# Products that fill half of TensorE's array, gathered into fewer bursts, in a one-core hybrid SSD and attention layer

## The chip, the core and the metric

The kernel runs on one core of a Trainium2 chip. The metric is the device time of one execution in microseconds (us), of which the median of three runs is given. The core has five instruction queues that meet only at semaphores: TensorE (PE, matrix products into PSUM; its weight loads are shown as PEld), VectorE (DVE), ScalarE (ACT), GpSimd (POOL) and SyncE (SP, which here issues nearly all DMAs). Each takes its instructions in the order in which they are written into its queue.

## The reference, cut to what matters

One layer on 512 tokens of width 1024, float32. `u = x @ w_in` is split into the inputs of two branches:

```python
# branch A, per direction; groups g = 4, heads per group r = 8, chunks c of 128 tokens
y_diag = einsum('bgcls,bgrcls,bcsgrp->bclgrp', cb, lmat, xc)     # within a chunk
y_off  = einsum('bclgn,bcgrpn,bgrcl->bclgrp', cc, prev, exp(a_cs))  # from the states before it
y = (y_f + y_b + d_skip * xh) * silu(z)        # both directions; then RMSNorm per group, @ w_proj_ssd
# branch B: 12 heads of width 64, windows with dilation 1, 4 and 16
o = einsum('bdhinm,bdhime->bdhine', softmax(q @ k.T / 8 - slope * dist), v)   # @ w_proj_attn
h = layer_norm(alpha * x + (sigmoid(gA) * A + sigmoid(gB) * B) @ w_out)
out = layer_norm(alpha * h + square(relu(h @ w_up)) @ w_down)
```

A head is 64 wide, and the array has 128 rows and 128 columns. So a product that sums over one head's width (the scores q k) fills 64 rows, and one that makes one head's output (y, and the products of softmax weights and values) fills 64 columns. The two heads of a pair are issued alternately, one on each half.

## The kernel before

The wide products (w_in, the projections, the two layers of the MLP) are made of 128 x 128 by 128 x 512 steps, each taken three times from a high and a low part of both operands (`mm3`, lines 136 to 138). The weights come from HBM through `Stream`: a DMA to `wraw`, ACT makes the high part `wh` (line 110), DVE the low part `wl` (line 111), with two buffers of `wh` and `wl`.

**SSD stage** (about 78 to 498 us). For each of four groups, `ssd(g)` runs beside a list of projection tiles (`tile_task`). Both are Python generators that yield an estimate of their time; `run` takes steps from the one that is behind, and this alone sets the order on TensorE (`tc.manual_schedule`). The order on the other engines is made by the framework's scheduler when the program is built.

In `ssd(g)` four pairs of heads follow each other (`pr`, each with tile `j = 4g + pr`). A pair loads two `bc` tiles and one `be` tile by DMA, makes the state products `ps_yo` (line 483) that DVE multiplies into `be` (lines 484 to 486), POOL adds the two directions' parts (line 487), and `head` builds each head's decay matrix `G1`, with four buffers (lines 444 to 465). One pair later, `y_out` (line 353) multiplies it by the transposed `x` (line 360: 8 products, 128 x 64 by 128, in the trace 16 records) into a PSUM tile of tag `y`, of which there are two. DVE adds `D * x` (line 362, into a tile `yt`), POOL adds `be` (line 363), DVE multiplies by the gate (line 364), ACT squares (line 366) and POOL sums the squares (line 368). The fourth pair's `y_out` waits in `late` for the next group's start.

**Attention stage** (498 to 590 us). `attention()` runs beside the projection tiles of branch A (`ps_pa`). Score products for the near window (line 628): for each of two tiles `i` of q and k, two bursts `bp` of four products, into two PSUM tiles each, `bp = 0` of tag `tp` (three buffers) and `bp = 1` of tag `y` (two buffers); then DVE adds the bias out of PSUM into `pt` (line 636), and takes maxima (line 637) and their negatives (line 639); ACT makes the exponentials. The scores with dilation (line 658) are four bursts of eight products, one for each of the tiles 2 to 5, loaded into the two buffers of q and k by `load_qk`. The score tiles are read from PSUM by DVE alone.

Then the weights are transposed on TensorE and multiplied with the values: `class_v` (line 716, 16 products, one burst for each `i`) and `near_v` (line 744, 4 products for each of four blocks `b`). `later()` issues what the previous step left in `todo`, so a burst of value products follows each set of transposes. Blocks 0 and 3 of `near_v` have two products whose sum runs over 64 rows only. The copies `tt` of the transposes rotate through six buffers.

Of the kernel before, what the change touches and what calls it, by code (L numbers as in the profile page):

```python
# [45 lines left out]
def hybrid_layer_kernel(ctx: ExitStack, tc: tile.TileContext, t: dict, out: bass.AP):  # L46
# [303 lines left out]
        for j in range(4 * g, 4 * g + 4):  # L350
            dve.scalar_tensor_tensor(ys[j], ys[j], vec[:, V_NW + j:V_NW + j + 1], ps, op0=ALU.mult, op1=ALU.mult)

    def y_out(g, pr, xt, ms, be, sqs):

        j = 4 * g + pr
        py = ps_tile("y", f"ps_y{j}", 2)
        for c in range(NCH):
            for hh in range(2):
                hs = slice((pr * 2 + hh) * HD, (pr * 2 + hh + 1) * HD)
                pe.matmul(py[hh * HD:(hh + 1) * HD, ch(c)], xt[c][:, hs], ms[hh][:, ch(c)], start=True, stop=True)  # L360
        yt = sp.tile([P, S], F32, name=f"yt{j}", tag="acc", bufs=2)
        dve.scalar_tensor_tensor(yt, fm["x", j], vec[:, V_DSK + j:V_DSK + j + 1], py, op0=ALU.mult, op1=ALU.add)
        pool.tensor_add(yt, yt, be[:, 0, :])
        dve.tensor_mul(ys[j], ys[j], yt)
        sq = sp.tile([P, S], F32, name=f"sq{j}", tag="sq", bufs=2)
        act.activation(sq, ys[j], AF.Square)
        if pr:
            pool.tensor_add(sq, sq, sqs[-1])
        sqs.append(sq)
        tail[g] = sq  # L370

    late = [None]

    def ssd(g):
# [17 lines left out]
            cb.append(cbm)  # L392
        yield 3.0 if g else 10.0
        if late[0]:
            y_out(*late[0])
        yield 1.5
        xt = []
        for c in range(NCH):
# [45 lines left out]
        def head(pr, hh, bcs):  # L444

            h = g * 8 + pr * 2 + hh
            U = sp.tile([P, S], F32, name=f"U{h}", tag="U", bufs=2)
            G1 = sp.tile([P, S], F32, name=f"G1_{h}", tag="G1", bufs=4)
            for c in range(NCH):
                act.activation(U[:, ch(c)], bcs[1][:, hh, ch(c)], AF.Identity, bias=acr[:, c, 32 + h:33 + h])  # L450
            for c in range(NCH):
                dve.scalar_tensor_tensor(U[:, ch(c)], bcs[0][:, hh, ch(c)], acr[:, c, h:h + 1], U[:, ch(c)], op0=ALU.subtract, op1=ALU.min)  # L452
            act.activation(U, U, AF.Exp)
            for c in range(NCH):
                act.activation(G1[:, ch(c)], cb[0][:, c, :], AF.Copy, scale=tok[:, c, h:h + 1])
# [12 lines left out]
        pend = None  # L468
        for pr in range(4):
            h0 = g * 8 + pr * 2  # L470
            j = 4 * g + pr
# [13 lines left out]
            dve.tensor_mul(be[:, 0, :P], be[:, 1, :P], po[1][:, :P])  # L485
            dve.tensor_mul(be[:, 1, P:S - P], be[:, 1, P:S - P], po[1][:, P:S - P])
            pool.tensor_add(be[:, 0, P:S - P], be[:, 0, P:S - P], be[:, 1, P:S - P])
            ms = []
            with tc.issue_after(ins.ins):
                ms.append(head(pr, 0, bcs))  # L490
            yield 7.0
            if pend:
                y_out(*pend)
            ms.append(head(pr, 1, bcs))
            yield 7.0
            pend = (g, pr, xt, ms, be, sqs)
# [73 lines left out]
    def attention():  # L570
# [23 lines left out]
        tts = [ap.tile([P, 4, P], F32, name=f"tt{n}", tag="tt", bufs=2) for n in range(2)]  # L594
# [22 lines left out]

        for i in range(2):
            qf, kf = qk[i]
            for bp in range(2):  # L620
                pss = pair_tiles(bp, f"ps_s0_{i}{bp}")
                for bb in range(2):
                    b = bp * 2 + bb
                    k0, k1 = kr[b]
                    o = k0 - (P * b - 64)
                    for hh in range(2):
                        pr = slice(hh * HD, (hh + 1) * HD)
                        pe.matmul(pss[hh][:, bb * 256 + o:bb * 256 + o + k1 - k0], qf[pr, b * P:(b + 1) * P], kf[pr, k0:k1], start=True, stop=True)
                for hh in range(2):
                    jj = 2 * i + hh  # L630
                    for bb in range(2):
# [6 lines left out]
                        nm = nm0[:, b, jj:jj + 1]  # L638
                        dve.tensor_scalar(nm, st0[:, b, 0, jj:jj + 1], -1.0, None, op0=ALU.mult)
                        act.activation(pt[:, :w], pt[:, :w], AF.Exp, bias=nm, accum_out=st0[:, b, 1, jj:jj + 1])  # L640
                yield 3.5
        dma.dma_start(vc, dr_v.rearrange("(i r) d -> i r d", r=4)[:, :, 0:512])
        dma.dma_start(v0[:, 1:4, :], dr_v[64:448, 512:768].rearrange("(c p) d -> p c d", p=P))
        dma.dma_start(v0[0:64, 0, :], dr_v[0:64, 512:768])
        dma.dma_start(v0[0:64, 4, :], dr_v[448:512, 512:768])
        dma.dma_start(dr_st.rearrange("(b p) m -> p b m", p=P), st0.rearrange("p b a j -> p b (a j)"))
        for gg in range(2):
            for i in range(2):
                tl = 2 + gg * 2 + i
                tile_qk(tl)  # L650
                load_qk(tl)
                qf, kf = qk[tl]
                pss = pair_tiles(i, f"ps_s{tl}")
                for r in range(4):
                    rs = slice(r * P, (r + 1) * P)
                    for hh in range(2):
                        pr = slice(hh * HD, (hh + 1) * HD)
                        pe.matmul(pss[hh][:, rs], qf[pr, rs], kf[pr, rs], start=True, stop=True)
                for hh in range(2):
                    jj = i * 2 + hh  # L660
                    pt = ptc[gg, jj]
# [99 lines left out]
        for i in range(2):  # L761
# [431 lines left out]
```

## Time and profile before

| | |
|---|---|
| median of three runs | 1011.24 us (1010.66 to 1011.32) |
| the profiled execution: time | 1010.76 us |
| its span in the profile | 1008.9 us |
| TensorE busy | 999.4 us (99%) |
| TensorE weight loads busy | 827.1 us |
| VectorE busy | 733.3 us (73%) |
| ScalarE busy | 548.3 us (54%) |
| GpSimd busy | 73.7 us (7%) |
| mean granted clock | 0.998 |

The profile is of one execution; rows below are from it, in us from the start of its span. Matmuls overlap, so the time that a matmul takes up is read from the distance between starts, and not from its duration. In a row of the timeline, neighbours of one kind are merged, with their count at the end.

### The profile page before, as it was taken

How to read it: one execution, taken by the hardware profiler on the slowest of the kernel's cores; microseconds unless marked ns; L12 is line 12 of the kernel's file. 1: busy time of each engine (PE TensorE's matmuls, PEld its weight loads, DVE VectorE, ACT ScalarE, POOL GpSimd, SP SyncE). 2: the span in 40 equal slices, each digit the busy share in tenths (PEclk: the TensorE clock that was granted, in tenths of full speed). 3: DMA queues.
4: the chain of work that ended last, by engine and by line, in shares of the span. 5: the costliest groups of instructions: out<-in, count | busy, mean ns of one | idle time of the engine just before them, and what ended most of it. 6: DMA issues, size and time to landing. Idle time of an engine off the chain costs nothing.

```text
span 1008.9 us, 13601 instructions
## 1 busy us (share of the span) xinstructions
PE 999.4 (99%) x5073; PEld 827.1 (82%) x5073; DVE 733.3 (73%) x1108; ACT 548.3 (54%) x1026; POOL 73.7 (7%) x66
## 2 busy tenths in 40 slices
PE   9999999999999999999999999999999999999997
PEld 7888888888888888888778778898888888888886
DVE  4296978679878996986698267564676886787457
ACT  4454787368857884765765444214544545454330
POOL 0000202220221122213000000000000000000000
PEclk9999999999999999999999999999999999999999
DMA  7435355434652555365774249414234314311222
GB/s 241 151 130 157 99 190 174 140 108 138 197 171 91 175 190 165 122 204 168 251 220 115 73 160 309 149 43 149 81 104 126 105 46 162 107 48 56 84 84 84
DMA packets 48450, 140.43 MB, mean 139 GB/s; under 512 B 6528, under 2 KB 7424, under 8 KB 48128
## 3 DMA queue, kind: packets, MB, share of 16 engines
q1 hardware_dynamic: 48240, 139.30, 43.4%
q8 instruction: 40, 0.66, 0.3%
q10 hardware_dynamic: 144, 0.26, 0.1%
q14 instruction: 26, 0.21, 0.1%
HBM read 128.25 MB, written 11.30 MB: 138 GB/s over the span
## 4 chain that ended last, share of the span: by engine, by line
PE 89%; DVE 5%; DMA 2%; ACT 2%; issue 1%; POOL 0%; DVEq 0%; SPq 0%; ACTq 0%; POOLq 0%
PE ps_u L137 6%; PE ps_u L138 6%; PE ps_u L136 6%; PE ps_p L136 4%; PE ps_p L138 4%; PE ps_p L137 4%; PE ps_pa L136 3%; PE ps_z L136 3%; PE ps_z L138 3%; PE ps_z L137 3%; PE ps_pa L137 3%; PE ps_pa L138 3%; PE ps_x L136 3%; PE ps_x L138 2%; PE ps_x L137 2%; PE ps_yo L483 2%
## 5 line engine op out<-in xcount | busy, mean ns | idle before, releaser
L111 DVE TENSOR_TENSOR wl<-wraw,wh 128x1024 fp32r<-128x1024 f32 (+1 forms) x141 | 172.0, 1223 | 123.1 <-ACT wh L110 118.7
L110 ACT CAST wh<-wraw 128x1024 fp32r<-128x1024 f32 (+1 forms) x141 | 145.9, 1039 | 192.4 <-PE ps_u L137 89.0
L137 PE MATMUL ps_u<-htl,wh 128*128 128x512 f32 (+1 forms) x288 | 105.3, 366 | 0.3 <-DVE htl L906 0.3
L136 PE MATMUL ps_u<-hth,wh 128*128 128x512 f32 (+1 forms) x288 | 105.3, 366 | 0.0
L138 PE MATMUL ps_u<-hth,wl 128*128 128x512 f32 (+1 forms) x288 | 105.2, 365 | 0.0
L1000 DVE TENSOR_TENSOR cl<-wq,ch 128x1024 fp32r<-128x1024 f32 x42 | 51.3, 1223 | 29.3 <-ACT ch L999 29.2
L136 PE MATMUL ps_p<-ch,ah 128*128 128x512 f32 x168 | 65.4, 389 | 0.0
L137 PE MATMUL ps_p<-cl,ah 128*128 128x512 f32 x168 | 65.4, 389 | 0.0
L138 PE MATMUL ps_p<-ch,al 128*128 128x512 f32 x168 | 65.4, 389 | 0.0
L137 PEld LDWEIGHTS ps_u<-htl,wh 128*128 128x128 f32 x288 | 54.3, 189 | 9.2 <-DVE htl L906 0.5
L138 PEld LDWEIGHTS ps_u<-hth,wl 128*128 128x128 f32 x288 | 54.3, 189 | 8.8
L136 PEld LDWEIGHTS ps_u<-hth,wh 128*128 128x128 f32 x288 | 54.2, 189 | 8.8 <-ACT hth L905 0.3
L999 ACT CAST ch<-wq 128x1024 fp32r<-128x1024 f32 x42 | 44.1, 1052 | 21.4 <-PE ps_p L138 21.4
L452 DVE SCALAR_TENSOR_TENSOR U<-bc,acr,U 128x128 f32<-128x128 f32 x128 | 45.9, 392 | 8.8 <-ACT U L450 8.7
L136 PE MATMUL ps_pa<-yh,wh 128*128 128x512 f32 x128 | 52.1, 407 | 0.0
L136 PE MATMUL ps_g<-xh,wh 128*128 128x512 f32 x128 | 51.5, 402 | 0.0
L136 PE MATMUL ps_x<-xh,wh 128*128 128x512 f32 x128 | 50.9, 398 | 0.0
L136 PE MATMUL ps_z<-xh,wh 128*128 128x512 f32 x128 | 50.9, 398 | 0.0
L137 PE MATMUL ps_pa<-yl,wh 128*128 128x512 f32 x128 | 50.1, 392 | 0.2 <-DVE yl L563 0.2
L138 PE MATMUL ps_g<-xh,wl 128*128 128x512 f32 x128 | 50.0, 391 | 0.1
L138 PE MATMUL ps_pa<-yh,wl 128*128 128x512 f32 x128 | 50.1, 391 | 0.0
L138 PE MATMUL ps_x<-xh,wl 128*128 128x512 f32 x128 | 50.1, 391 | 0.0
(289 smaller groups left out, 2444.7 us busy)
## 6 DMA issues: line engine op xcount, KB each, us to landing
wraw<-in_w_in_dram SPq DMA_DIRECT2D x68, 512.0 KB, 3.6
bc<-dr_acr SPq DMA_DIRECT2D x32, 512.0 KB, 4.3
wraw<-in_w_up_dram SPq DMA_DIRECT2D x32, 512.0 KB, 3.6
wq<-in_w_dn_dram SPq DMA_DIRECT2D x24, 512.0 KB, 4.4
be<-dr_ear SPq DMA_DIRECT2D x32, 256.0 KB, 4.6
wraw<-in_w_ps_dram SPq DMA_DIRECT2D x16, 512.0 KB, 4.0
dr_gate<-g SPq DMA_DIRECT2D x16, 256.0 KB, 2.1
wraw<-in_w_out_dram SPq DMA_DIRECT2D x8, 512.0 KB, 4.7
```

The source lines that it names most:

```text
L110: act.copy(h[:, :width], r[:, :width])
L111: dve.tensor_sub(l[:, :width], r[:, :width], f32(h[:, :width]))
L136: pe.matmul(ps, lh, rh, start=(first and i == 0), stop=False)
L137: pe.matmul(ps, lh, rl, start=False, stop=False)
L138: ins = pe.matmul(ps, ll, rh, start=False, stop=(last and i == n - 1))
L452: dve.scalar_tensor_tensor(U[:, ch(c)], bcs[0][:, hh, ch(c)], acr[:, c, h:h + 1], U[:, ch(c)], op0=ALU.subtract, op1=ALU.min)
L483: pe.matmul(po[d][:, ch(c)], prev[d, c][:, pr * P:(pr + 1) * P], C[:, ch(c)], start=True, stop=True)
L999: act.copy(h, w[:, j, :])
L1000: dve.tensor_sub(l, w[:, j, :], f32(h))
```

## The change

Four things. `y_out` takes a list of pairs, makes the y products of all of them first and then does their elementwise work; in each group it is called with pairs 0 and 1 (while pair 2 is under way) and with pairs 2 and 3 (at the next group's start). Since two pairs wait longer, the `G1` tiles of pairs 2 and 3 take the buffers of `xwh` and `xwl`. The sum `D * x + be` is formed in place in `x` on DVE as soon as `be` is there; `y_out` then only adds the product to it (DVE) and multiplies by the gate, and POOL's addition is gone.

In the scores, four PSUM tiles are taken and all products into them are issued as one burst, before any of the DVE work: for the near window those of one `i`, for the dilated ones those of two tiles, both of which are loaded before. The value products wait until block 2, so that `class_v` with blocks 0 and 1, and blocks 2 and 3, are a burst each; the copies `tt` rotate through seven buffers.

```diff
-    def y_out(g, pr, xt, ms, be, sqs):
+    def y_out(ys_):
...
+        for g, pr, xt, ms, sqs in ys_:
+            py = ps_tile("y", f"ps_y{4 * g + pr}", 2)
...
+            pys.append(py)
+        for (g, pr, xt, ms, sqs), py in zip(ys_, pys):
+            j = 4 * g + pr
+            yt = fm["x", j]
+            dve.tensor_add(yt, yt, py)
...
-        yt = sp.tile([P, S], F32, name=f"yt{j}", tag="acc", bufs=2)
-        dve.scalar_tensor_tensor(yt, fm["x", j], vec[:, V_DSK + j:V_DSK + j + 1], py, op0=ALU.mult, op1=ALU.add)
-        pool.tensor_add(yt, yt, be[:, 0, :])
...
-            G1 = sp.tile([P, S], F32, name=f"G1_{h}", tag="G1", bufs=4)
+            tag, bufs = (("G1", 4), ("G1", 4), ("xwh", 2), ("xwl", 2))[pr]
+            G1 = sp.tile([P, S], F32, name=f"G1_{h}", tag=tag, bufs=bufs)
...
             pool.tensor_add(be[:, 0, P:S - P], be[:, 0, P:S - P], be[:, 1, P:S - P])
+            dve.scalar_tensor_tensor(xs[pr], xs[pr], vec[:, V_DSK + j:V_DSK + j + 1], be[:, 0, :], op0=ALU.mult, op1=ALU.add)
...
-            if pend:
-                y_out(*pend)
+            if pr == 2:
+                y_out(pend)
+                pend = []
...
         for i in range(2):
             qf, kf = qk[i]
+            psb = [pair_tiles(bp, f"ps_s0_{i}{bp}") for bp in range(2)]
             for bp in range(2):
-                pss = pair_tiles(bp, f"ps_s0_{i}{bp}")
+                pss = psb[bp]
...
+            for bp in range(2):
+                pss = psb[bp]
                 for hh in range(2):
...
-                yield 3.5
+            yield 7.0
...
+                psb.append(pair_tiles(i, f"ps_s{tl}"))
+            for i in range(2):
+                qf, kf = qk[2 + gg * 2 + i]
+                pss = psb[i]
...
-                yield 4.0
+            yield 8.0
...
-            n = nt[0] % 6
+            n = nt[0] % 7
...
                 yield 2.4
-                later()
+                if b == 2:
+                    later()
```

**TensorE, group 1, the y products.** Before, the burst of pair 0 (`G_8`, `G_9`) stands alone between two rows of a projection tile:

```order
L137 MATMUL ps_x_2355<-xl_117,wh_2317 128x512
L138 MATMUL ps_x_2355<-xh_109,wl_2318 128x512
L360 MATMUL ps_y_2362<-G_8_2143,xt_0_1866 64x128
L360 MATMUL ps_y_2362<-G_9_2205,xt_0_1866 64x128
L360 MATMUL ps_y_2362<-G_8_2143,xt_1_1882 64x128
L360 MATMUL ps_y_2362<-G_9_2205,xt_1_1882 64x128
L360 MATMUL ps_y_2362<-G_8_2143,xt_2_1902 64x128
L360 MATMUL ps_y_2362<-G_9_2205,xt_2_1902 64x128
L360 MATMUL ps_y_2362<-G_8_2143,xt_3_1909 64x128
L360 MATMUL ps_y_2362<-G_9_2205,xt_3_1909 64x128
L136 MATMUL ps_x_2355<-xh_110,wh_2317 128x512
L137 MATMUL ps_x_2355<-xl_118,wh_2317 128x512
```

In the changed kernel the same place holds no y products, and where pair 1's burst (`G_10`, `G_11`) stood, some 70 rows on, pair 0's stands directly ahead of it (its last two rows are the first here):

```order
L361 MATMUL ps_y_2503<-G_8_2140,xt_3_1905 64x128
L361 MATMUL ps_y_2503<-G_9_2202,xt_3_1905 64x128
L361 MATMUL ps_y_2512<-G_10_2292,xt_0_1862 64x128
L361 MATMUL ps_y_2512<-G_11_2361,xt_0_1862 64x128
L361 MATMUL ps_y_2512<-G_10_2292,xt_1_1878 64x128
L361 MATMUL ps_y_2512<-G_11_2361,xt_1_1878 64x128
L361 MATMUL ps_y_2512<-G_10_2292,xt_2_1898 64x128
L361 MATMUL ps_y_2512<-G_11_2361,xt_2_1898 64x128
L361 MATMUL ps_y_2512<-G_10_2292,xt_3_1905 64x128
L361 MATMUL ps_y_2512<-G_11_2361,xt_3_1905 64x128
L136 MATMUL ps_x_2490<-xh_112,wh_2411 128x512
L137 MATMUL ps_x_2490<-xl_120,wh_2411 128x512
```

Eight such bursts of 16 products take the place of sixteen of 8.

**TensorE, the near scores of the second q and k tile.** Before, with what each row waits for in brackets, only `bp = 0` (`ps_s_10`) is issued here, and projection products follow; `bp = 1` (`ps_s_11`) comes 16 rows after the first of these:

```order
L138 MATMUL ps_pa_4947<-yh_4762,wl_4891 128x512
L628 MATMUL ps_s_10_0_4994<-k_4839,q_4838 128x192 [waits DMAHW6_49,DMAHW5_49,PE_49]
L628 MATMUL ps_s_10_1_4995<-k_4839,q_4838 128x192 [waits DVE_49]
L628 MATMUL ps_s_10_0_4994<-k_4839,q_4838 128x256
L628 MATMUL ps_s_10_1_4995<-k_4839,q_4838 128x256
L136 MATMUL ps_pa_5022<-yh_4755,wh_4943 128x512 [waits Activation_49]
L137 MATMUL ps_pa_5022<-yl_4771,wh_4943 128x512
```

In the changed kernel `bp = 1` follows at once, with its two waits on DVE:

```order
L138 MATMUL ps_pa_4954<-yh_4746,wl_4876 128x512
L635 MATMUL ps_s_10_0_4979<-k_4823,q_4822 128x192 [waits DMAHW6_49,DMAHW5_49,PE_49]
L635 MATMUL ps_s_10_1_4980<-k_4823,q_4822 128x192 [waits DVE_49]
L635 MATMUL ps_s_10_0_4979<-k_4823,q_4822 128x256
L635 MATMUL ps_s_10_1_4980<-k_4823,q_4822 128x256
L635 MATMUL ps_s_11_0_4981<-k_4823,q_4822 128x256 [waits DVE_49]
L635 MATMUL ps_s_11_1_4982<-k_4823,q_4822 128x256 [waits DVE_49]
L635 MATMUL ps_s_11_0_4981<-k_4823,q_4822 128x192
L635 MATMUL ps_s_11_1_4982<-k_4823,q_4822 128x192
L136 MATMUL ps_pa_5029<-yh_4739,wh_4950 128x512 [waits Activation_49]
L137 MATMUL ps_pa_5029<-yl_4755,wh_4950 128x512
```

The waits are the same; the twelve projection products between the two bursts have moved behind both. What the waits are for are the additions on DVE that read the PSUM tiles `ps_s_01` of the first q and k tile out of the two buffers of tag `y`. On DVE they stand so, before:

```order
L636 TENSOR_TENSOR pt_02_4833<-ps_s_01_0_4954,b_4869 128x256
L637 TENSOR_REDUCE st_4860<-pt_11_4836 128x1
L637 TENSOR_REDUCE st_4860<-pt_02_4833 128x1
L639 TENSOR_SCALAR nm_4862<-st_4860 128x1
L636 TENSOR_TENSOR pt_03_4834<-ps_s_01_0_4954,b_4869 128x192
L639 TENSOR_SCALAR nm_4862<-st_4860 128x1
L111 TENSOR_TENSOR wl_5019<-wraw_4888,wh_5018 128x1024
L637 TENSOR_REDUCE st_4860<-pt_03_4834 128x1
L636 TENSOR_TENSOR pt_12_4837<-ps_s_01_1_4955,b_4869 128x256
L639 TENSOR_SCALAR nm_4862<-st_4860 128x1
L636 TENSOR_TENSOR pt_13_4840<-ps_s_01_1_4955,b_4869 128x192
```

and now:

```order
L646 TENSOR_REDUCE st_4845<-pt_11_4820 128x1
L645 TENSOR_TENSOR pt_02_4817<-ps_s_01_0_4900,b_4854 128x256
L648 TENSOR_SCALAR nm_4847<-st_4845 128x1
L645 TENSOR_TENSOR pt_03_4818<-ps_s_01_0_4900,b_4854 128x192
L646 TENSOR_REDUCE st_4845<-pt_02_4817 128x1
L646 TENSOR_REDUCE st_4845<-pt_03_4818 128x1
L111 TENSOR_TENSOR wl_5026<-wraw_4873,wh_5025 128x1024
L648 TENSOR_SCALAR nm_4847<-st_4845 128x1 x2
L645 TENSOR_TENSOR pt_12_4821<-ps_s_01_1_4901,b_4854 128x256
L645 TENSOR_TENSOR pt_13_4824<-ps_s_01_1_4901,b_4854 128x192
```

Counted from the `wl` step that the trace of before has at 495.65 us, and from the one that answers to it in the changed kernel, up to the last of these eight additions, DVE has the same 3 `wl` steps, 12 low parts `yl`, 8 additions, 6 maxima and 6 negatives; the order among neighbours differs, and the last addition stands at the end in both.

**VectorE, group 1.** Before, pair 0's `yt` step reads the product, POOL adds `be` to it, and two rows later the gate's product waits for POOL:

```order
L288 SCALAR_TENSOR_TENSOR x_2265<-x_2265,acc_2266 128x512
L362 SCALAR_TENSOR_TENSOR yt_2371<-x_1181,vec,ps_y_2362 128x512
L452 SCALAR_TENSOR_TENSOR U_2377<-bc_1_0_2274,acr,U_2377 128x128
L463 TENSOR_TENSOR G_11_2378<-G_11_2378,G_11_2392 128x512
L364 TENSOR_TENSOR y_87<-y_87,yt_2371 128x512
L464 TENSOR_TENSOR G_11_2378<-G_11_2378,U_2377 128x512
```

Now the step with `x` and `be` (line 492, here pair 1's) stands shortly behind the last step that writes `be`, with one step between them in which POOL adds:

```order
L489 TENSOR_TENSOR be_1_2275<-be_1_2275,ps_yo_1_2279 128x128
L286 SCALAR_TENSOR_TENSOR acc_2263<-ps_x_2237,vec,acc_2263 128x511
L490 TENSOR_TENSOR be_1_2275<-be_1_2275,ps_yo_1_2279 128x256
L286 SCALAR_TENSOR_TENSOR acc_2263<-ps_x_2237,vec,acc_2263 128x511
L492 SCALAR_TENSOR_TENSOR x_1353<-x_1353,vec,be_1_2275 128x512
L286 SCALAR_TENSOR_TENSOR acc_2263<-ps_x_2237,vec,acc_2263 128x510
```

The wait on POOL has moved from `yt` to `be`.

## Rows read from the trace of the kernel before

**Rows 1.** The page: busy time, share and instructions of each engine; and the shares of the chain of work that ended last, by engine.

```profile
PE 999.4 (99%) x5073; PEld 827.1 (82%) x5073; DVE 733.3 (73%) x1108; ACT 548.3 (54%) x1026; POOL 73.7 (7%) x66
...
PE 89%; DVE 5%; DMA 2%; ACT 2%; issue 1%; POOL 0%; DVEq 0%; SPq 0%; ACTq 0%; POOLq 0%
```

**Rows 2.** Busy time of each engine in three stretches: the pairs of group 1, the pairs of group 3, the near scores. Columns: from and to, length, busy time (with the count) of PE, PEld, DVE, ACT and POOL, granted clock, DMA share, GB/s.

```profile
229.00:294.00 65.00, 65.00 (x351) 53.82 (x351) 60.22 (x105) 51.01 (x123) 11.80 (x9) 1.00 0.55 172
...
420.00:470.00 50.00, 49.90 (x282) 40.88 (x283) 42.48 (x94) 32.85 (x80) 7.71 (x8) 1.00 0.61 199
498.00:515.00 17.00, 17.00 (x88) 12.36 (x87) 16.76 (x49) 10.12 (x29) 0.00 (x0) 1.00 0.94 305
```

**Rows 3.** Timeline of TensorE around one burst of y products (line 360) between products of a projection tile: start, duration, engine, line, out<-in, shape, count.

```profile
249.70 0.39 PE L138 MATMUL ps_x<-xh,wl 128*128 128x512 f32 x1
...
250.38 0.39 PE L138 MATMUL ps_x<-xh,wl 128*128 128x512 f32 x1
250.70 1.09 PE L360 MATMUL ps_y<-G,xt 128*64 128x128 f32 x16
251.72 0.50 PE L136 MATMUL ps_x<-xh,wh 128*128 128x512 f32 x1
...
252.52 0.40 PE L136 MATMUL ps_x<-xh,wh 128*128 128x512 f32 x1
```

**Rows 4.** The same view: the value products of `class_v`, twice as many in one burst.

```profile
553.38 1.97 PE L716 MATMUL ps_ac<-tt,vc 128*64 128x128 f32 x32
```

**Rows 5.** The same view: four transposes alone; then the bursts of `near_v` for block 0 (two of its products sum over 64 rows) and block 1, which four transposes follow.

```profile
543.97 0.39 PE L138 MATMUL ps_pa<-yh,wl 128*128 128x512 f32 x1
544.20 0.60 PE L705 MATMUL ps_pt<-tri,pt 128*128 128x128 f32 x4
...
545.34 0.40 PE L136 MATMUL ps_pa<-yh,wh 128*128 128x512 f32 x1
...
558.62 0.81 PE L744 MATMUL ps_an<-tn,v 64*64 64x128 f32 x8
...
561.01 0.39 PE L138 MATMUL ps_pa<-yh,wl 128*128 128x512 f32 x1
561.33 0.66 PE L744 MATMUL ps_an<-tn,v 128*64 128x128 f32 x8
...
563.11 0.39 PE L136 MATMUL ps_pa<-yh,wh 128*128 128x512 f32 x1
```

**Rows 6.** The same view: the two near score bursts of the second q and k tile (line 628), and one burst of dilated scores (line 658).

```profile
508.08 1.03 PE L628 MATMUL ps_s<-k,q 64*128 64x192 f32 x8
509.04 0.50 PE L136 MATMUL ps_pa<-yh,wh 128*128 128x512 f32 x1
...
511.99 1.03 PE L628 MATMUL ps_s<-k,q 64*128 64x256 f32 x8
...
515.57 0.39 PE L138 MATMUL ps_pa<-yh,wl 128*128 128x512 f32 x1
515.88 1.16 PE L658 MATMUL ps_s<-k,q 64*128 64x128 f32 x16
...
517.78 0.39 PE L136 MATMUL ps_pa<-yh,wh 128*128 128x512 f32 x1
```

**Rows 7.** Timeline of VectorE in the near scores: the low parts of weights (line 111) and the fourth to eighth additions that read the first q and k tile's scores from PSUM (line 636).

```profile
495.65 1.22 DVE L111 TENSOR_TENSOR wl<-wraw,wh 128x1024 fp32r<-128x1024 f32 x1
...
507.68 0.75 DVE L636 TENSOR_TENSOR pt<-ps_s,b 128x256 f32<-128x256 f32 x2
...
509.05 0.35 DVE L636 TENSOR_TENSOR pt<-ps_s,b 128x192 f32<-128x192 f32 x1
...
509.38 1.22 DVE L111 TENSOR_TENSOR wl<-wraw,wh 128x1024 fp32r<-128x1024 f32 x1
...
510.77 0.42 DVE L636 TENSOR_TENSOR pt<-ps_s,b 128x256 f32<-128x256 f32 x1
...
511.16 0.35 DVE L636 TENSOR_TENSOR pt<-ps_s,b 128x192 f32<-128x192 f32 x1
```

**Rows 8.** Groups of instructions: line, engine, operation, out<-in, shapes, count | busy us, mean ns of one | idle time before them and what ended it. Two steps on the y products; one step of three operands in SBUF; one addition out of PSUM; POOL's addition.

```profile
L362 DVE SCALAR_TENSOR_TENSOR yt<-x,vec,ps_y 128x512 f32<-128x512 f32 x16 | 11.8, 739 | 1.9 <-PE ps_y L360 1.9
L364 DVE TENSOR_TENSOR y<-y,yt 128x512 f32<-128x512 f32 x16 | 11.0, 690 | 15.5 <-POOL yt L363 15.5
...
L288 DVE SCALAR_TENSOR_TENSOR C<-C,acc 128x512 f32<-128x512 f32 x4 | 2.7, 685 | 0.0
...
L751 DVE TENSOR_TENSOR ac<-ac,ps_an 128x512 f32<-128x512 f32 x2 | 1.4, 688 | 3.3 <-PE ps_an L744 3.3
...
L363 POOL TENSOR_TENSOR yt<-yt,be 128x512 f32<-128x512 f32 x16 | 21.9, 1366 | 92.2 <-DVE yt L362 84.6 <-ACT x L287 7.6
```

**Rows 9.** Waits of SP's DMA queue: the loads of `be` (line 479) on POOL's `yt`: us in total, times, longest us.

```profile
SPq L479 <- POOL yt L363: 44.8, 13, 6.7
```

**Rows 10.** Timeline of TensorE in group 3, two neighbouring products of a projection tile.

```profile
448.97 0.39 PE L137 MATMUL ps_g<-xl,wh 128*128 128x512 f32 x1
449.46 0.50 PE L138 MATMUL ps_g<-xh,wl 128*128 128x512 f32 x1
```

**Rows 11.** DMA issues from 495 to 545 us: the loads of k, count, size of one, median us from issue to landing.

```profile
k<-dr_qk SPq DMA_DIRECT2D x5, 256.0 KB, 4.3
```

**Rows 12.** Timeline of TensorE at the start of the span: warm-up products.

```profile
1.19 4.21 PE L190 MATMUL ps_warm<-warm 128*128 128x512 bf16 x11 [1.19 <-DVE warm L187]
```

More of the change, by code (lines that the diff above doesn't have):

```diff
@@ L351, in norm @@
             dve.scalar_tensor_tensor(ys[j], ys[j], vec[:, V_NW + j:V_NW + j + 1], ps, op0=ALU.mult, op1=ALU.mult)
-    def y_out(g, pr, xt, ms, be, sqs):
[L355 to L360, printed above, removed]
-        yt = sp.tile([P, S], F32, name=f"yt{j}", tag="acc", bufs=2)
-        dve.scalar_tensor_tensor(yt, fm["x", j], vec[:, V_DSK + j:V_DSK + j + 1], py, op0=ALU.mult, op1=ALU.add)
-        pool.tensor_add(yt, yt, be[:, 0, :])
[L364 to L370, printed above, removed]
+    def y_out(ys_):
+        pys = []
+        for g, pr, xt, ms, sqs in ys_:
+            py = ps_tile("y", f"ps_y{4 * g + pr}", 2)
+            for c in range(NCH):
+                for hh in range(2):
+                    hs = slice((pr * 2 + hh) * HD, (pr * 2 + hh + 1) * HD)
+                    pe.matmul(py[hh * HD:(hh + 1) * HD, ch(c)], xt[c][:, hs], ms[hh][:, ch(c)], start=True, stop=True)
+            pys.append(py)
[3 more added lines that the diff above has]
+            dve.tensor_add(yt, yt, py)
+            dve.tensor_mul(ys[j], ys[j], yt)
+            sq = sp.tile([P, S], F32, name=f"sq{j}", tag="sq", bufs=2)
+            act.activation(sq, ys[j], AF.Square)
+            if pr:
+                pool.tensor_add(sq, sq, sqs[-1])
+            sqs.append(sq)
+            tail[g] = sq
     late = [None]
@@ L394, in ssd @@
         if late[0]:
-            y_out(*late[0])
+            y_out(late[0])
         yield 1.5
@@ L467, in ssd @@
         sqs = []
-        pend = None
+        pend = []
         for pr in range(4):
@@ L491, in ssd @@
             yield 7.0
-            if pend:
-                y_out(*pend)
+            if pr == 2:
+                y_out(pend)
+                pend = []
             ms.append(head(pr, 1, bcs))
             yield 7.0
-            pend = (g, pr, xt, ms, be, sqs)
+            pend.append((g, pr, xt, ms, sqs))
         late[0] = pend
@@ L523, in hybrid_layer_kernel @@
             run(ssd(g), bg(mix[g][:rest]), 86.5 if g else 93.5, 4 * QT * rest)
-        y_out(*late[0])
+        y_out(late[0])
         for n, (k, j) in enumerate(mix[3][rest:]):
@@ L593, in attention @@
         ptc = {(gg, jj): ap.tile([P, 4, P], F32, name=f"pt{gg}_{jj}") for gg in range(2) for jj in range(4)}
-        tts = [ap.tile([P, 4, P], F32, name=f"tt{n}", tag="tt", bufs=2) for n in range(2)]
+        tts = [ap.tile([P, 4, P], F32, name=f"tt{n}", tag="tt", bufs=3) for n in range(3)]
         st0 = ap.tile([P, NCH, 2, 4], F32, name="st0")
@@ L647, in attention @@
         for gg in range(2):
+            psb = []
             for i in range(2):
@@ L651, in attention @@
                 load_qk(tl)
-                qf, kf = qk[tl]
-                pss = pair_tiles(i, f"ps_s{tl}")
+                psb.append(pair_tiles(i, f"ps_s{tl}"))
+            for i in range(2):
+                qf, kf = qk[2 + gg * 2 + i]
+                pss = psb[i]
                 for r in range(4):
@@ L658, in attention @@
                         pe.matmul(pss[hh][:, rs], qf[pr, rs], kf[pr, rs], start=True, stop=True)
+            for i in range(2):
+                pss = psb[i]
                 for hh in range(2):
@@ L693, in tt_tile @@
             nt[0] += 1
-            n = nt[0] % 6
+            n = nt[0] % 7
             if n < 4:
                 return (aq, ap)[n // 2].tile([P, 4, P], F32, name=name, tag=("q0", "k0", "q1", "k1")[n], bufs=1)
-            return ap.tile([P, 4, P], F32, name=name, tag="tt", bufs=2)
+            return ap.tile([P, 4, P], F32, name=name, tag="tt", bufs=3)
         def class_t(i, hh, gg):
```

## Prediction

> **What bounds the kernel now.** I read the page's engine shares and the chain of work first, since they say which engine's time is the kernel's time. TensorE is busy for 99% of the span and the chain that ended last lies on it for 89%; VectorE is at 73%, GpSimd at 7% [rows 1]. An average hides stages, so next I read three stretches: in group 1 DVE is busy 60.22 of 65 us, in group 3 42.48 of 50, and in the near scores 16.76 of 17 while TensorE has no idle time that shows [rows 2]. So TensorE's stream sets the end everywhere, and in the near scores DVE is full as well. GpSimd is never near its limit. What is taken out of TensorE's stream is a gain, and a wait that is put into it a loss, one for one.
>
> How much of TensorE's time a burst takes is the distance between starts. In a plain stretch three products of 512 columns take 250.38 − 249.70 = 0.68 us, 0.227 each [rows 3]. A burst's price is what remains when these steps are taken off the distance between two of them around it.
>
> **The change part by part: y products.** From 250.38 to 252.52 there are a burst of 16 records and four plain steps (the one at 250.38 and the three from 251.72 on): 2.14 − 4 x 0.227 = 1.23 us for the burst [rows 3]. The 16 records more in a burst of 32 add 1.97 − 1.09 = 0.88 us [rows 3, 4]. So a burst that joins another costs 0.35 us less than alone: that is what the switch from full-array to half-array work and back takes. Sixteen bursts become eight: 8 x 0.35 = −2.8 us, all on TensorE.
>
> **Scores.** The dilated burst costs 517.78 − 515.57 − 4 x 0.227 = 1.30 us [rows 6]; less the same 0.88 this is 0.42 a merge. The near bursts of the same size in columns take the same price. Eight bursts become four: 4 x 0.42 = −1.7 us, before waits.
>
> **Values.** A near burst with four transposes costs 563.11 − 561.01 − 0.91 = 1.19 us, the transposes alone 545.34 − 543.97 − 0.91 = 0.46 [rows 5]. That leaves 0.73 for eight records; at half of 0.88 they cost 0.44 inside a burst, so 0.29 is what a removed burst returns. Nine bursts become four: 5 x 0.29 = −1.45. The 64-row products of block 0 now stand inside longer bursts; I charge each tile the difference in duration, 0.81 − 0.66 = 0.15 [rows 5], twice: +0.3. Together −1.15. The three parts give −5.65, of which I keep −5.6 us.
>
> **The new wait.** The merged near burst of the second q and k tile needs both PSUM buffers of tag `y`, which the first tile's `ps_s_01` holds until DVE's fifth to eighth additions have read it. Before, that second half came at 511.99 [rows 6], just after the eighth addition ended at 511.16 + 0.35 = 511.5 [rows 7]. Now it follows the first half directly: 508.08, less one merge (0.42), plus the 0.96 from 508.08 to 509.04 [rows 6], is 508.6. The eighth addition can't come sooner: from the `wl` at 495.65 to it DVE has the same work in both kernels, with hardly a gap (16.76 of 17 us [rows 2]). That the scores arrive earlier doesn't help a full engine. So TensorE waits 511.5 − 508.6 = 2.9 us. Behind the waiting product stand the twelve projection products that filled this time before; they can't pass it. Nothing later gives it back, as TensorE is the bound to the end: +2.9. Bounds: 0, if DVE gets the additions in ahead of the `wl` steps of 1.22 us each that stand between them [rows 7] and more; about 4, if one more `wl` gets ahead.
>
> A page speaks against the gain here: the Trainium skill, "TensorEngine Tiling (Array Packing)", section PSUM Bottleneck, says that tiling speeds up the products but not the emptying of PSUM, which may then be the limit. By that rule alone the scores' 1.7 us would buy nothing; the rows above let the y and value parts pass, since their PSUM tiles have time, and show the limit at one burst.
>
> After it, the first dilated merged burst needs the loads of tile 3. They are issued once the second near burst has freed the buffer, at about 512.5, and take 4.3 us [rows 11]: 516.8 for a need at about 517.9. I cost this at nothing; at one and a half times that landing time the wait would be 1.1 us.
>
> **The SSD stage's other engines.** DVE gets 16 more steps with `x` and `be`: a step of three SBUF operands is 685 ns, the addition out of PSUM 688, the `yt` step that goes 739 [rows 8]: 16 x (0.685 + 0.688 − 0.739) = +10.1 us of DVE work. Against it stand the 15.5 us that DVE sat before the gate's product, waiting for POOL's 1.37 us addition [rows 8], which goes, with 21.9 us of POOL. The new wait, for POOL's addition into `be`, has one DVE step between. By stretch DVE has 65 − 60.22 = 4.8 us to spare in group 1 and 7.5 in group 3 [rows 2], for 4 x 0.634 = 2.5 us more in each group: it fits. In SP's queue the `be` loads waited 44.8 us for POOL's `yt`, 13 times [rows 9]; the products that follow from a pair's loads come no later than now, and one stall of TensorE in group 3 (0.49 instead of 0.227 [rows 10]) may go. The y products run later than before and so find their decay matrices ready. I take 0 for all this; bounds −0.3 (that stall) and, if the whole DVE addition of groups 1 to 3 lands on TensorE, 12 x 0.634 = +7.6.
>
> **Sum.** −5.6 + 2.9 = −2.7 us. The profiled execution took 1010.76 us, so 1008.0; the median lies 0.48 above it, so I predict 1008.5.
>
> **The rivals.** *No wait in the near scores.* DVE reads `ps_s_01` early enough. For: the merged first burst gives it the scores some 3 us sooner. Against: DVE has no idle time there to use. The time is 1011.24 − 5.6 = 1005.6.
>
> *The clock falls.* TensorE would idle for 3 us in the near scores; in the stretches of the trace it hardly idles at all, and the granted clock is 1.00 [rows 2]. If it goes down to 1.2 GHz, the price is bounded by the warm-up: eleven products of 512 columns in 4.21 us instead of 11 x 0.227 = 2.50 [rows 3, 12], +1.7, and 1010.2. The Trainium skill, "TensorE: Matmul & The Clock Gate", section HAM oscillation, states that the clock goes back to half when TensorE has idled for some time; no row of this trace shows that.
>
> *DVE becomes the bound in groups 1 to 3, slower than before.* The `be` steps are put on DVE ahead of the decay matrices, which TensorE's y products need, and the merged `late` burst brings four elementwise steps at a group's start ahead of the work for the state products. If all of the 7.6 us lands on TensorE, the time is 1016.1. It decides once more than 4.7 us of it lands (2.7 eaten, 2 beyond). Against: 4.8 us to spare per 65 us and the 15.5 us that go.
>
> *The gain is eaten by small waits.* Loads of tiles 3 to 5 land late by 1.1 us once or twice, or the value bursts wait for their copies `tt`: 1009.6 to 1011, within the measurement.
>
> *The joined bursts cost no less.* The change then doesn't do what it says, and only the wait, +2.9, is left: 1014.1. The 1.97 us of 32 records, less than twice the 1.09 of 16 [rows 3, 4], speaks against it.
>
> **How the numbers follow.** Forecast (1007.3 to 1009.5 with the wait between 2 and 4 us): 56%. No wait: 14%. Clock: 6%. Small waits: 15%. DVE bound: 8%. Joined bursts that cost no less: 1%. A measurement of this kernel tells some 0.2%, 2 us, from no change: faster is below 1009.2. Of the forecast 50 of 56 lie below that, with all 14 of no wait and 2 from the clock case, 66%; slower are the last two cases, 9%; the rest is 25%. The range of 8 in 10 reaches from no wait with a little more from the edges, 1005.3, to the end of the small waits, 1011.5; it leaves out the DVE case, the joined bursts that cost no less and some of the tails.
>
> **What would show it.** Right: eight y bursts in the new trace, each 32 records of about 2 us, and about 0.35 us less per pair; a gap of TensorE of 2 to 4 us near 509, ended by DVE's `pt` step, before the second half of the near scores, with a granted clock of 1.00 behind it; no new idle time of TensorE in groups 1 to 3; DVE's wait on POOL's `yt` gone, with less on `be`. Wrong: no gap at 509 (the first rival), TensorE waiting for `xwh`, `G` or `bth` in groups 1 to 3 (the DVE rival), products that take twice as long after the gap (the clock), or a merged burst that is as long as two.

## The result and the profile after

The changed kernel takes 1012.85 us (median of 22 executions, 1010.09 to 1014.80) against 1010.68 us before (22 executions): a ratio of 1.0018, 95% interval 1.0011 to 1.0025. It is 2.2 us slower, where 2.7 us less had been forecast, and outside the range. The span's granted clock was 0.998 in 4 of the 22 executions (1010.1 to 1010.7 us) and 0.995 to 0.997 in the others (1011.2 to 1014.8 us). By clock, the medians are 1010.4 us at 0.998 (4 executions), 1012.7 at 0.996 or 0.997 (10) and 1013.7 at 0.995 (8). The profiled execution took 1011.71 us, with 0.996; that of before had 0.998.

Two lines of the page of the changed kernel, engines and chain, which answer to [rows 1]:

```profile
PE 997.3 (99%) x5073; PEld 830.1 (82%) x5073; DVE 737.0 (73%) x1124; ACT 547.7 (54%) x1026; POOL 51.8 (5%) x50
...
PE 88%; DVE 6%; ACT 3%; DMA 2%; issue 1%; POOL 0%; DVEq 0%; SPq 0%; ACTq 0%
```

TensorE is less busy and the span is longer: the time went into waits and, as rows further down show, into slower products. The waits of TensorE in the changed kernel (line, releaser, us, times, longest):

```profile
PE ps_s L635 <- DVE pt L645: 2.2, 2, 1.7
...
PE ps_g L138 <- DVE wl L111: 1.0, 1, 1.0
PE ps_st L137 <- DVE xwl L423: 0.5, 2, 0.3
```

The stretches of [rows 2] and two behind the near scores, in the changed kernel:

```profile
229.00:294.00 65.00, 65.00 (x360) 54.48 (x359) 60.39 (x110) 49.27 (x119) 6.38 (x5) 1.00 0.58 187
420.00:470.00 50.00, 48.97 (x282) 40.69 (x282) 42.52 (x98) 33.06 (x78) 4.67 (x5) 1.00 0.65 204
498.00:515.00 17.00, 14.80 (x70) 11.08 (x71) 16.88 (x53) 10.05 (x30) 0.00 (x0) 0.90 0.92 314
511.00:516.00 5.00, 5.00 (x18) 3.69 (x16) 5.00 (x25) 4.04 (x16) 0.00 (x0) 0.67 0.62 213
...
512.00:514.00 2.00, 2.00 (x6) 1.60 (x6) 2.00 (x11) 1.48 (x7) 0.00 (x0) 0.50 0.58 220
```

Group 1 is as full as before. In group 3 TensorE now stands idle for a microsecond, in the near scores for 2.2 us, and behind these its granted clock is 0.67 on average over 5 us. From 512 to 514 it is 0.50, the lower of its two levels (1.2 instead of 2.4 GHz).

The timeline of TensorE there, with the idle time before an instruction and its releaser in brackets:

```profile
506.31 0.39 PE L138 MATMUL ps_pa<-yh,wl 128*128 128x512 f32 x1
506.63 1.03 PE L635 MATMUL ps_s<-k,q 64*128 64x192 f32 x8
508.11 0.70 PE L635 MATMUL ps_s<-k,q 64*128 64x256 f32 x2 [0.45 <-DVE pt L645]
510.55 1.53 PE L635 MATMUL ps_s<-k,q 64*128 64x256 f32 x6 [1.74 <-DVE pt L645]
512.01 0.80 PE L136 MATMUL ps_pa<-yh,wh 128*128 128x512 f32 x1
512.60 0.63 PE L137 MATMUL ps_pa<-yl,wh 128*128 128x512 f32 x1
513.03 0.63 PE L138 MATMUL ps_pa<-yh,wl 128*128 128x512 f32 x1
...
514.31 0.41 PE L138 MATMUL ps_pa<-yh,wl 128*128 128x512 f32 x1
514.56 0.39 PE L136 MATMUL ps_pa<-yh,wh 128*128 128x512 f32 x1
```

From 512.60 to 514.31 the full products follow each other at 0.43 us, not 0.227, and return to speed at 514.3. The releaser is the pair of additions at 509.81 in DVE's timeline, whose last ends at 510.49, with the `wl` step of 1.22 us right ahead of it, as forecast from [rows 7]:

```profile
507.71 0.35 DVE L645 TENSOR_TENSOR pt<-ps_s,b 128x192 f32<-128x192 f32 x1
...
508.56 1.22 DVE L111 TENSOR_TENSOR wl<-wraw,wh 128x1024 fp32r<-128x1024 f32 x1
...
509.81 0.68 DVE L645 TENSOR_TENSOR pt<-ps_s,b 128x256 f32<-128x256 f32 x2
```

The joined bursts themselves came out as priced. A joined y burst, of 32 records, in the timeline of the changed kernel:

```profile
263.10 0.39 PE L138 MATMUL ps_x<-xh,wl 128*128 128x512 f32 x1
263.42 1.97 PE L361 MATMUL ps_y<-G,xt 128*64 128x128 f32 x32
265.31 0.50 PE L136 MATMUL ps_x<-xh,wh 128*128 128x512 f32 x1
...
266.11 0.40 PE L136 MATMUL ps_x<-xh,wh 128*128 128x512 f32 x1
```

From 263.10 to 266.11 are 3.01 us, less 4 x 0.227: 2.10 for two pairs, where [rows 3] gave 2 x 1.23.

DVE's steps on y, by line (busy us, mean ns, idle time ahead), which answer to [rows 8]:

```profile
L492 DVE SCALAR_TENSOR_TENSOR x<-x,vec,be 128x512 f32<-128x512 f32 x16 | 12.0, 747 | 3.9 <-POOL be L491 3.9
L367 DVE TENSOR_TENSOR y<-y,x 128x512 f32<-128x512 f32 x16 | 10.8, 688 | 0.2
L366 DVE TENSOR_TENSOR x<-x,ps_y 128x512 f32<-128x512 f32 x16 | 10.7, 681 | 3.2 <-PE ps_y L361 3.2
```

The wait on POOL went from 15.5 us to 3.9.

### The profile page after: what moved, and what is told of

It is laid out like the page before. It is cut to its first block, busy times and chain, and to the rows that moved or that the text cites. A ratio compares the mean times of both kernels' runs of the same rounds, so it can differ in the third digit from the quotient of the medians.

```text
span 1009.9 us, 13585 instructions
## 1 busy us (share of the span) xinstructions
PE 997.3 (99%) x5073; PEld 830.1 (82%) x5073; DVE 737.0 (73%) x1124; ACT 547.7 (54%) x1026; POOL 51.8 (5%) x50
## 4 chain that ended last, share of the span: by engine, by line
PE 88%; DVE 6%; ACT 3%; DMA 2%; issue 1%; POOL 0%; DVEq 0%; SPq 0%; ACTq 0%
PE ps_u L137 6%; PE ps_u L138 6%; PE ps_u L136 6%; PE ps_p L137 4%; PE ps_p L138 4%; PE ps_p L136 4%; PE ps_z L136 3%; PE ps_z L138 3%; PE ps_z L137 3%; PE ps_pa L136 3%; PE ps_pa L138 3%; PE ps_pa L137 3%; PE ps_x L138 2%; PE ps_x L136 2%; PE ps_x L137 2%; PE ps_yo L487 2%
## 5 line engine op out<-in xcount | busy, mean ns | idle before, releaser
L138 PE MATMUL ps_z<-xh,wl 128*128 128x512 f32 x128 | 49.9, 390 | 0.0
```

The source lines that it names most:

```text
L138: ins = pe.matmul(ps, ll, rh, start=False, stop=(last and i == n - 1))
```

## The experiments

Each kernel's median stands beside that of the kernel before from the same chip.

| kernel | us | before | ratio (95%) |
|---|---|---|---|
| near_split | 1007.53 | 1010.78 | 0.9967 (0.9954 to 0.9979) |
| near_fill | 1009.97 | 1010.78 | 0.9991 (0.9983 to 1.0000) |
| y_only | 1009.95 | 1010.78 | 0.9994 (0.9985 to 1.0003) |
| att_only | 1012.89 | 1010.78 | 1.0019 (1.0010 to 1.0027) |
| sq_in_x | 1007.34 | 1010.42 | 0.9974 (0.9965 to 0.9983) |
| be_after | 1009.14 | 1010.42 | 0.9988 (0.9979 to 0.9996) |
| inplace | 1009.98 | 1010.42 | 0.9996 (0.9987 to 1.0005) |
| best | 1007.53 | 1010.42 | 0.9976 (0.9966 to 0.9985) |
| near_first | 1008.03 | 1011.21 | 0.9971 (0.9960 to 0.9982) |
| g3_apart | 1007.67 | 1011.21 | 0.9961 (0.9950 to 0.9973) |
| bc3 | 1005.44 | 1011.21 | 0.9942 (0.9930 to 0.9954) |
| near_split_2 | 1007.73 | 1011.21 | 0.9963 (0.9951 to 0.9975) |
| apart_bc3 | 1007.96 | 1010.41 | 0.9976 (0.9966 to 0.9986) |
| bc3_2 | 1005.42 | 1010.41 | 0.9950 (0.9937 to 0.9962) |

**near_split** puts the near scores back to four bursts:

```diff
-            psb = [pair_tiles(bp, f"ps_s0_{i}{bp}") for bp in range(2)]
             for bp in range(2):
-                pss = psb[bp]
+                pss = pair_tiles(bp, f"ps_s0_{i}{bp}")
...
-            yield 7.0
+                yield 3.5
```

> The changed kernel with the near scores put back to four bursts of four products, as before; the y products, dilated scores and value products stay joined. Theory 1 (the wait of TensorE for DVE's fifth to eighth additions, and the fall of the clock behind it, eat the gain): the gap of 2.2 us near 508 and the slow products behind it go, the two joins of 0.42 us are lost; 1007.5 to 1009.5 us, 3.3 to 5.3 below the changed kernel's 1012.85, granted clock 0.998 in every run. Rival (the SSD stage eats it, through DVE's 16 more steps): only the joins are lost, 1013.5.

1007.53, with a clock of 0.998 in all five executions. One joined place out of four kinds had cost more than all the others gave.

**near_fill** keeps the near scores joined, and gives TensorE something to do in the wait:

```diff
+                if i and bp:
+                    for _ in range(9):
+                        pe.matmul(fill, yh[0][:, :P], yh[1], start=True, stop=True)
```

> The changed kernel with nine more products of 512 columns between the two halves of the second near burst, into a PSUM tile that nobody reads: 9 x 0.227 = 2.0 us of work in the place of the 2.2 us in which TensorE waited. If the idle time is what brings the clock down, the end of the wait stays where it was and the products behind it run at 0.227 us: the granted clock is 0.998 in every run and the time 1009.5 to 1011. Rival (the clock falls for another reason, such as the longer half-array bursts, which are all still there): the clock falls as often as before, 1012.5 to 1013.2.

1009.97, with 0.998 or 0.999 in all eleven executions (1008.4 to 1010.6). Its timeline of TensorE, and the stretch behind the burst:

```profile
506.11 0.39 PE L138 MATMUL ps_pa<-yh,wl 128*128 128x512 f32 x1
506.43 1.03 PE L640 MATMUL ps_s<-k,q 64*128 64x192 f32 x8
507.39 2.33 PE L633 MATMUL ps_fill<-yh,yh 128*128 128x512 f32 x9
509.65 1.70 PE L640 MATMUL ps_s<-k,q 64*128 64x256 f32 x8
511.28 0.50 PE L136 MATMUL ps_pa<-yh,wh 128*128 128x512 f32 x1
...
512.07 0.40 PE L136 MATMUL ps_pa<-yh,wh 128*128 128x512 f32 x1
```

```profile
511.00:516.00 5.00, 5.00 (x24) 3.95 (x23) 5.00 (x24) 4.12 (x16) 0.00 (x0) 1.00 0.60 200
```

The work added is nine products, the end of the wait hardly moves, and the clock is 1.00. The fill also splits a long half-array burst; but the joined burst of the first tile, as long and without a wait, stands in near_first and best below, with a clock of 0.998 or 0.999 in all 17 executions. So it was the idle time that brought the clock down.

This gives both prices. The clock: 1.0018 − 0.9991 = 0.0027 of 1010.7, 2.7 us. The wait: the burst costs 512.07 − 506.11 − 4 x 0.227 = 5.05 us, and the joined near burst of the first tile in the same trace, where nothing waits, 500.20 − 497.35 − 4 x 0.227 = 1.94: 3.1 us.

```profile
497.35 0.40 PE L138 MATMUL ps_pa<-yh,wl 128*128 128x512 f32 x1
497.68 1.78 PE L640 MATMUL ps_s<-k,q 64*128 64x192 f32 x16
499.39 0.50 PE L136 MATMUL ps_pa<-yh,wh 128*128 128x512 f32 x1
...
500.20 0.39 PE L136 MATMUL ps_pa<-yh,wh 128*128 128x512 f32 x1
```

Of the 3.1 us, 0.4 is the change between full and half array that the fill itself adds (two separate near bursts cost 2 x 1.16 us in the kernel before). So the wait alone is 2.7, and the clock up to 3.1; their sum, 5.8, doesn't depend on the split. near_split shows it from the other side: 1.0018 − 0.9967 is 5.2 us, and the two joins given up are 0.8 more, 6.0.

**y_only** and **att_only** have one stage of the changed kernel each, and the other of the kernel before.

> The SSD stage of the changed kernel with the attention stage of the kernel before. Theory 1: eight joins of y bursts give 2.9 us, and the waits that the trace shows in group 3 (the state products near 400, a projection product near 461) give back some 1.9: 1009.7 (1009.0 to 1010.5). Rival (the SSD stage is where the change loses): 1011 or more.

> The SSD stage of the kernel before with the attention stage of the changed one. Theory 1: near scores +2.2 for the wait, +2 to 4 for the clock, -0.43 for the first joined burst; dilated scores -0.83; value products -1.15: 1012.4 to 1014.5, with the fall of the clock in most runs. Rival (the SSD stage is where the change loses): 1009 or less.

1009.95 and 1012.89: the loss lies in the attention stage, but the SSD stage yields 0.8 where its joins alone were priced at 2.9. In att_only the clock was below 0.998 in seven of eleven executions.

**inplace** leaves every burst as before and moves only the sum onto DVE:

```diff
-        dve.scalar_tensor_tensor(yt, fm["x", j], vec[:, V_DSK + j:V_DSK + j + 1], py, op0=ALU.mult, op1=ALU.add)
-        pool.tensor_add(yt, yt, be[:, 0, :])
+        yt = fm["x", j]
+        dve.tensor_add(yt, yt, py)
...
+            dve.scalar_tensor_tensor(xs[pr], xs[pr], vec[:, V_DSK + j:V_DSK + j + 1], be[:, 0, :], op0=ALU.mult, op1=ALU.add)
```

> The kernel before, with D * x + be in place in x on DVE and POOL's addition gone, and nothing joined. Theory: DVE's 16 more steps cost TensorE nothing by themselves, but the loads of be move ahead of bc in SP's queue as in the changed kernel: a wait of about 1 us near 461, 1010.8 to 1011.9. Rival 1 (DVE's work lands on TensorE): 1013 or more. Rival 2 (nothing is lost): 1010.4 to 1010.8, no wait near 461.

1009.98, and no wait near 449 or 461: the second rival, a little below its range. DVE's ten microseconds more land on no path. My theory on SP's queue fell here: in this kernel too pair 3's `be` is issued ahead of pair 2's second `bc`, without a wait.

So the joins bring the waits. In the changed kernel they stand where group 3 begins and in its last pair. ACT's timeline at both places:

```profile
395.52 0.63 ACT L369 ACTIVATE sq<-y 128x512 f32<-128x512 f32 x1 [1.77 <-POOL sq L371]
396.06 1.06 ACT L406 COPY xt<-ps_xt 128x512 f32<-128x512 f32 x2
...
455.31 0.99 ACT L454 ACTIVATE U<-bc,acr 128x128 f32<-128x128 f32 x3 [3.88 <-DMA bc<-dr_acr]
456.20 0.62 ACT L369 ACTIVATE sq<-y 128x512 f32<-128x512 f32 x1
...
459.23 1.05 ACT L110 CAST wh<-wraw 128x1024 fp32r<-128x1024 f32 x1
```

At the first, the second late pair's square waits for a buffer that POOL frees, and the copies `xt`, from which the state products come, stand behind it. At the second, the weights' high part stands behind steps that wait for a load of `bc`; TensorE wants its low part at 461.1 and gets it at 462.26:

```profile
460.84 0.39 PE L137 MATMUL ps_g<-xl,wh 128*128 128x512 f32 x1
462.26 0.50 PE L138 MATMUL ps_g<-xh,wl 128*128 128x512 f32 x1 [1.03 <-DVE wl L111]
```

**sq_in_x** (on near_split) tests the first:

```diff
-            sq = sp.tile([P, S], F32, name=f"sq{j}", tag="sq", bufs=2)
+            sq = yt
```

> The kernel of near_split, with ACT's squares written into the tile of x, which has been used up, instead of into one of two buffers of tag sq. Theory: the wait of TensorE for the state products near 400 (0.25 + 0.50 + 0.11 us) comes from ACT's queue, in which the second late pair's square waits for GpSimd's sum to free a buffer, with the copies of xt behind it; without that wait it goes, 1006.2 to 1007.0. Rival (the two additions more on DVE at the group's start delay xw by themselves): the wait stays, 1007.5.

By distances the wait near 400 went from 0.86 us to 0.2, as said, but its trace has a new one of 1.0 near 381 (products waiting for `wl`), and 1007.34 is no gain. **be_after** and **best** load `be` behind `bc`; `best` has the squares in x and the first near burst joined as well:

```diff
+            with tc.issue_after(bd.ins):
+                for hh in range(2):
+                    dma.dma_start(be[hh * HD:(hh + 1) * HD], ...
```

> The kernel of near_split, with the loads of be issued behind both loads of bc of their pair. Theory: the wait of TensorE near 461 (0.62 + 0.11 us in near_split, 1.19 + 0.11 in the changed kernel) comes from SP's queue, in which pair 3's be now stands ahead of pair 2's second bc, since its buffer is free sooner; with bc first, bc lands sooner, ACT waits less ahead of the weights' high part, and the wait goes: 1006.5 to 1007.2. Rival (bc is late because its own buffers are freed late): the wait stays, 1007.5.

> Squares in x, be behind bc, and in the near scores the four products bursts of the first q and k tile joined, those of the second apart. If the parts add up: 1007.5 - 0.9 - 0.7 - 0.43 = 1005.5 (1004.8 to 1006.3), with a granted clock of 0.998 or more. Rival (DVE frees the buffers of tag y too late for the second tile's second burst, which now comes 0.4 us sooner): a short wait of TensorE near 509, 1006 to 1006.5.

The wait near 461 went in both, yet be_after is slower than near_split, 1009.14, and its executions spread from 1007.0 to 1011.3: the order of loads only moved the waits (0.3 us near 441, and 1.4 us for ACT's `xt` near 300, where the trace of att_only, with the SSD stage of before, has one of 1.0). `best` gives 1007.53: the parts don't add up.

**g3_apart** was meant to take the join of pairs 0 and 1 out of group 3 alone. Its condition holds for pair 3 too, so the join of pairs 2 and 3 goes as well: the trace has four bursts of 16 records there, at 437.11, 449.23, 461.35 and 468.04 us. **near_first** joins the first near burst alone; **near_split_2** repeats near_split beside them.

```diff
-            if pr == 2:
+            if pr == 2 or (pend and g == 3):
```

> The kernel of near_split with the y products of group 3's pairs 0 and 1 apart, as before (pairs 2 and 3 of all groups and pairs 0 and 1 of groups 0 to 2 stay joined). A join less costs 0.36. Theory (in group 3 the weights' high part stands in ACT's queue behind steps that wait for the load of bc, and the joined stream of TensorE gets to those weights before they are ready): the wait near 461 (0.73 in near_split) shrinks to 0.2 or less, and the time stays at 1007.2 to 1007.8. Rival (the wait comes from the in-place sums on DVE): the wait stays, 1007.9.

> The kernel of near_split with the near scores of the first q and k tile joined again, those of the second apart. If a join is worth 0.42 us wherever its PSUM buffers are free: 1007.1 (0.4 below near_split), no wait of TensorE between 497 and 512. Rival (the second tile's burst now comes before DVE has freed the buffers of tag y): a wait near 509, no gain, 1007.5 or more.

> The kernel of near_split again, beside the three others on one chip: 1007.2 to 1007.8; small waits of TensorE in groups 2 and 3 may stand at other places than in its first trace if the landing of loads sets them, and at the same places if the order of the queues alone does.

g3_apart: the wait near 461 is gone, and the time, 1007.67 beside 1007.73, is that of near_split although two joins are gone and not one: of their price, 0.7 us, nothing shows in group 3. near_first, 1008.03, gains nothing either: no wait arises near 509, but the first dilated burst waits in its place. Its timeline:

```profile
513.84 1.16 PE L671 MATMUL ps_s<-k,q 64*128 64x128 f32 x16
515.21 1.16 PE L671 MATMUL ps_s<-k,q 64*128 64x128 f32 x16 [0.21 <-DVE pt L646]
516.30 0.50 PE L136 MATMUL ps_pa<-yh,wh 128*128 128x512 f32 x1
```

By distances that burst costs 2.67 us instead of 2.20: what the join gave, 0.4, goes at the next place where DVE has to empty PSUM. The repeat of near_split has a wait near 381 that its first trace hasn't, with the order of the queues the same: in the SSD stage something that differs between executions sets where TensorE waits. That it is the landing of loads, as the expectation has it, is not shown.

**bc3** (on sq_in_x) gives `bc` a third buffer, out of the memory of `sq`:

```diff
-                b2 = sp.tile([P, 2, S], F32, name=f"bc{g}_{pr}_{d}", tag="bc", bufs=2)
+                b2 = sp.tile([P, 2, S], F32, name=f"bc{g}_{pr}_{d}", tag="bc", bufs=3)
```

> The kernel of sq_in_x with three buffers of bc instead of two (the memory of tag sq pays for it), so that one load of the next pair can be issued before this pair's decay matrices are done. Theory (the load of bc, which waits for its buffer, sets ACT's queue and so the weights): ACT's wait on bc in group 3 falls from 8 or 9 us, TensorE's wait near 461 goes, 1006.4 to 1007.0. Rival (the transfers are the limit: more of them at a time land later): the waits stay or move, 1007.3 or more.

1005.44, 0.9942 of the kernel before, and 1005.42 in the repeat, the fastest of all and better than forecast. ACT's waits between 400 and 470 us, first of the kernel before, then of near_split, then of bc3:

```profile
ACT U L450 <- DMA bc<-dr_acr: 10.4, 3, 4.7
```

```profile
ACT U L454 <- DMA bc<-dr_acr: 8.6, 2, 4.8
```

```profile
ACT U L454 <- DMA bc<-dr_acr: 4.6, 2, 3.9
```

So the wait for `bc` isn't new with the change; in the kernel before it cost TensorE no more than the 0.3 us of [rows 10]. All waits of TensorE in bc3, in which none on `wl` in groups 1 to 3 is left:

```profile
PE ps_warm L190 <- DVE warm L187: 1.2, 1, 1.2
PE ps_st L137 <- DVE xwl L423: 0.4, 1, 0.4
PE ps_u L137 <- DVE htl L918: 0.3, 1, 0.3
PE ps_pa L137 <- DVE yl L569: 0.2, 1, 0.2
```

**apart_bc3** is bc3 with every y burst alone (`if pend:` in the place of `if pr == 2:`), to see whether the buffer helps by itself.

> The kernel of bc3 with all y products apart, a burst for each pair, as before the change; in-place sums, three buffers of bc and the attention stage of near_split stay. If a joined y burst is worth its 0.36 us once the loads of bc don't hold up the stream: 8 x 0.36 = 2.9 above bc3, 1008.3 (1007.9 to 1008.7). Rival (the third buffer helps by itself, and the joins are worth the 0.8 us that y_only showed): 1006.2 (1005.8 to 1006.7).

> The kernel of bc3 again, beside apart_bc3 on one chip: 1005.0 to 1006.0.

1007.96 beside 1005.42: with the third buffer the eight joins are worth 2.5 us, near their price of 2.9. In the traces the first near burst starts at 498.32 in apart_bc3 and at 495.70 in bc3_2; with two buffers, joins move it only from 498.24 (inplace) to 497.82 (y_only). Without the joins the buffer has little to save: attention with its joins (−2.4, near_split less y_only) and the in-place sums (−0.4) account for apart_bc3's −2.45 within the noise.

## Why the prediction was wrong

*The prices of the joins* held. By distances the eight y joins save 2.9 us (2.8 forecast), the two dilated ones 0.8, the first near one 0.4; all bursts of the value products with their transposes fall by some 1.1 us, near the −1.15 of the sum.

*The new wait* held in place, cause and size: 2.7 us alone, or 3.1 with the lost join, in near_fill, against 2.9, released by the eighth addition. The Trainium skill's rule on emptying PSUM ("TensorEngine Tiling (Array Packing)", PSUM Bottleneck) agrees with that, and with near_first, where the saved time is lost at the next PSUM tile.

*The clock* is the step that failed first. The prediction kept it at full speed in the forecast and gave its fall 6% and 1.7 us, bounded by the warm-up. It fell in 18 of 22 executions, and cost 2.7 us on the median (2.2 to 3.3 by the medians of the executions with a lower clock, less that at 0.998). The row it leant on, a clock of 1.00 in stretches where TensorE hardly idles [rows 2], says nothing of a stretch with a wait of 3 us: a wait that the sum itself put there. The Trainium skill's statement on idle time ("TensorE: Matmul & The Clock Gate", HAM oscillation) agrees in that idle time brings the clock down, as near_fill shows. The idle stretches here, 0.45 and 1.74 us, are shorter than the waits for loads of that section's example, and the measurement decides.

*"I take 0 for all this"* is the step that failed second. The SSD stage gave 0.8 us where the sum had 2.8 to 2.9 for it. DVE's work, the one price worked out there, was rightly put at nothing (inplace). What was missed is that a stream which TensorE runs through faster wants its weights earlier, while ACT, which makes their high part, waits for loads of `bc` that come when one of their two buffers is free. The claim that "the products that follow from a pair's loads come no later than now" looked at the loads alone, and not at what stands behind them in ACT's queue. bc3 and apart_bc3 show it: with a third buffer the joins give 2.5 us, without it about 0.4 (y_only against inplace, a difference within their noise of some 0.9).

Together: −5.65 + 3.1 + 2.7 + 2.1 = +2.2 us, and 2.2 were measured. That they agree so well is in part luck: the 2.7 is itself the distance to near_fill, so what the sum tests is near_fill, −0.45 against −0.8 measured; and y_only and att_only, −0.8 and +2.1, add up to +1.3 and not +2.2. Both lie within the intervals, some 0.9 us to either side. The mechanism of the forecast was right with its wait, and the two terms left out, 4.8 us, turned its sign.

Still open: why the clock stayed up in 4 of 22 executions, and why it was 0.997 in two of the eleven of sq_in_x, whose profiled execution, one of the other nine, has no such wait. The squares in x alone gain nothing (sq_in_x, 0.9974 beside near_split's 0.9967 and 0.9963), so bc3's gain comes with the buffer; the buffer without them is untried.

## What to carry to other kernels

Where the engine that has to empty the bursts is full, joining them can only move the wait, and here the idle wait of TensorE was paid a second time in clock: price a wait that you add with the clock behind it, or fill it. When the engine that sets the end gets faster, look at what its inputs wait for, in-order queues and buffer counts included: a gain that the loads can't follow isn't there until they have a buffer more. Undoing one join of four kinds (near_split) and adding one buffer, out of memory freed by the squares in x (bc3), took the change from 1.0018 to 0.9942 and 0.9950.

## What the runs showed of the hardware

In the profiled execution TensorE's granted clock fell to 0.50 (a mean of 0.67 over 5 us) behind two idle stretches of 0.45 and 1.74 us; full products then started 0.43 us apart, for some 2 us in this trace, and 0.227 again after it. With nine products that nobody reads in that wait it stayed at 1.00 (near_fill). Going from full-array to half-array products and back costs some 0.36 (y) to 0.4 us (scores) of TensorE's time for each burst: that is what joining two bursts of 8 or 16 records saved.
